# Rotary key by ScalarE, rotary tables by VectorE, first layer's second-attention queries made turned

## The chip, the cores and the metric

The kernel runs on one core of one Trainium2 chip. The metric is the device time of one execution in microseconds (us). Names of engines are those of the profile: PE (TensorE, the matrix engine) with PEld (its weight loads), DVE (VectorE), ACT (ScalarE), POOL (GpSimd), SP (SyncE, which issues the DMAs here). L234 means line 234 of the kernel before; line numbers of the changed kernel differ by up to some 30.

## The reference

A decoder trunk of two layers over one sequence of 256 tokens and 1024 features. Each layer normalises x, projects it once, runs three mixers on parts of the projection (MLA, MoBA and retention), gates and merges them, and adds a squared-ReLU MLP. What matters here:

```
h = rms_norm(x, g)
(cq, ckv, k_rope, mq, mk, mv, ...) = split(h @ w_in)

# first attention, MLA: 8 heads
q = rms_norm(cq) @ w_q_up      -> per head 64 plain + 32 rotary columns
kv = rms_norm(ckv) @ w_kv_up   -> per head 64 plain key + 64 value columns
k = concat(plain key, the one rotary key k_rope, turned by cos/sin, repeated for all heads)
o_mla = softmax(causal(q k^T / sqrt(96))) v

# second attention, MoBA: 8 heads of 64; one block of 256 tokens, so causal attention
q, k = rotary on the first 16 of 64 columns of each head of mq, mk
o_moba = softmax(causal(q k^T / 8)) mv
```

## The kernel before

Data layout. Activations lie "turned" (features on the 128 partitions, 256 tokens along the free dimension) or in "token form" (128 tokens on the partitions). Products are made in fp32r from operands split into a high and a low part: `three` (L234 to L236) issues high x high, high x low, low x high. Every weight block comes by a DMA that SP issues into a buffer `raw` (7 of them), ACT writes its high part `whi` (L213), DVE its low part `wlo` (L215; 6 buffers each). PSUM has eight banks: four for accumulators `acc`, four for all else (`misc`).

Order. The program is a list of units `prog` (one projection block each), and `at(slot, step)` hangs further work behind a unit. `trunk` runs the list, and a scheduler that estimates the time of every instruction then fixes the order on each engine, except where an order is kept by hand (`manual_schedule`, `keep_in_program_order`). The buffers of a pool are given out in rotation, so a change in what is allocated first changes who shares a buffer, or a PSUM bank, with whom.

First layer, start. While x arrives chunk by chunk, `start(k, mq)` (k = 0 to 7) multiplies chunk k by 416 columns for MLA (`b0`: cq, ckv, k_rope) and 512 columns for MoBA's queries (`mq`), in token form: L728, L729 and L731. Ahead of that, WARM = 8 products on constants (L634) run while the first loads come. `moba_done("mq")` scales the two query accumulators by the norm on ACT (L700), and `rope` turns their rotary columns on DVE (L441 to L444, four operations per 128 tokens, with the tables K_COS_MB, K_SIN_MB).

Keys of MoBA, and in the second layer its queries too, are made turned by `project_turned`: per weight block eight products of 512 columns (high weight by both parts of x, L393) and eight of 256 (low weight by the high part, L395); the two halves of the accumulator are added by an ACT copy `second` (L399) and a DVE add into `qkraw` (L400). `rope_turned` (L428 to L430) then multiplies by tables and swaps rows: `swapped` issues four DMAs per pair (L420). For MoBA all three operations run on POOL. `tables` scales the tables by the row of norms, two POOL products of 256 columns (L412), in both layers, and again for retention.

Because the first layer's `mq` are in token form, `moba_turn` (L882, L886) transposes them later, four PE transposes and one ACT copy for each of two groups, ahead of MoBA's scores.

MLA's projections. `c_turn` (L777 to L787) transposes the normalised compressed rows into two PSUM banks `pct`, splits them into `cTh` and `cTl` (L250, L251), and lays the turned rotary key into the key tensor `KK`, one 64-row half at a time: an ACT copy out of PSUM into `krT` (L785), and two DVE copies of it, each repeated for four heads (L786, L787). Then follow the units `qrope` (rotary query columns, copied by ACT as `qr`, L816, swapped by DMA), `qnope` (plain query columns, copied into `Q` by ACT, L801 and L802) and `kvup` (plain keys, copied into `KK` by DVE, L801 and L802 as well, and values `pv`). `qr_rope` (L834 to L838, DVE) turns the rotary query columns and adds them into `Q`. The scores of MLA (L857) need `Q` and `KK`.

## Time and profile before

| | |
|---|---|
| time, median of 3 runs | 835.89 us (835.47 to 836.11) |
| time of the profiled execution | 836.19 us |
| its span, first to last instruction | 834.4 us |
| mean granted TensorE clock | 0.998 |
| PE busy | 827.0 us |
| DVE, ACT, POOL busy | 587.0, 482.3, 93.2 us |
| weights and inputs read | 151.00 MB |

The times come from executions without the profiler, the rows from one execution with it. A row of the timeline has start, duration (us), engine, line, operation, the tile written and the tiles read, shape, and in brackets how long the engine was idle before and what ended that. A row of a group has the number of instructions and their least, median and largest duration in ns. "PE acc L234 <- DVE qkraw L400: 0.4, 1, 0.4" reads: PE at L234 waited for DVE's write of qkraw at L400, 0.4 us in total, once, 0.4 at most. Matmuls are pipelined: their rows overlap, and the distance from start to start is their pace.

### The profile page before, as it was taken

To read this page: it belongs to the slowest core of one execution; us is meant where nothing else is said; L and a number is where in the kernel's file an instruction comes from. 1 tells how busy PE (TensorE), PEld (TensorE's weight loads), DVE (VectorE), ACT (ScalarE), POOL (GpSimd) and SP (SyncE) were. 2 spreads that over 40 slices of the span, in tenths; PEclk is the share of its full clock that TensorE was granted. 3 is DMA by queue.
4 is the path that set the end of the run, shared out by engine and by line. 5 is a ranking of instruction groups with operands and counts; after the bars stand their busy time and mean duration, and the time that the engine had idled before them with its cause. 6 is when DMAs were issued, how large, how long until landed. Compare 5 with 4: busy or idle time off the path is not lost.

```text
span 834.4 us, 12139 instructions
## 1 busy us (share of the span) xinstructions
PE 827.0 (99%) x4366; PEld 701.2 (84%) x4366; DVE 587.0 (70%) x1062; ACT 482.3 (58%) x859; POOL 93.2 (11%) x80
## 2 busy tenths in 40 slices
PE   9999999999999999999999999999999999999997
PEld 7888878888888888888898888888888888888886
DVE  6879667595787666666699876766868775656663
ACT  7766765445556555555685575664545555555552
POOL 0221000040030000000057111002101200000000
PEclk9999999999999999999999999999999999999999
DMA  9956744646467566665565657446565656666611
GB/s 345 361 182 202 242 140 148 192 137 214 145 184 227 184 195 191 189 191 173 172 198 176 211 175 240 155 137 195 156 199 158 219 173 188 200 196 186 197 53 50
DMA packets 45708, 155.98 MB, mean 187 GB/s; under 512 B 5712, under 2 KB 6736, under 8 KB 45392
## 3 DMA queue, kind: packets, MB, share of 16 engines
q1 hardware_dynamic: 45072, 154.54, 58.6%
q8 instruction: 34, 0.56, 0.3%
q10 hardware_dynamic: 576, 0.67, 0.2%
q14 instruction: 26, 0.21, 0.1%
HBM read 151.00 MB, written 1.05 MB: 182 GB/s over the span
## 4 chain that ended last, share of the span: by engine, by line
PE 97%; DMA 1%; DVE 1%; ACT 0%; issue 0%; DVEq 0%
PE acc L234 18%; PE acc L236 18%; PE acc L235 18%; PE pup L1097 14%; PE pup L1099 7%; PE acc L1047 5%; PE acc L393 4%; PE acc L395 2%; PE ps_s L857 1%; PE ps_pt L496 1%; DMA raw<-wts 1%; PE po L523 1%; PE ps_s L462 1%; PE po L525 0%; PE pmt L1013 0%; PE ps_r L462 0%
## 5 line engine op out<-in xcount | busy, mean ns | idle before, releaser
L215 DVE TENSOR_TENSOR wlo<-raw,whi 128x1024 fp32r<-128x1024 f32 (+4 forms) x287 | 347.5, 1219 | 182.4 <-ACT whi L213 126.8
L213 ACT ACTIVATE whi<-raw 128x1024 fp32r<-128x1024 f32 (+4 forms) x287 | 292.4, 1025 | 188.3 <-PE acc L236 104.2
L1097 PE MATMUL pup<-xs,whi 128*128 128x512 f32 x504 | 123.3, 390 | 0.0
L234 PE MATMUL acc<-whi,xs 128*128 128x512 f32 (+1 forms) x304 | 119.6, 395 | 0.0
L236 PE MATMUL acc<-whi,xs 128*128 128x512 f32 (+1 forms) x304 | 119.3, 393 | 0.0
L235 PE MATMUL acc<-wlo,xs 128*128 128x512 f32 (+1 forms) x304 | 118.8, 391 | 0.0
L1097 PEld LDWEIGHTS pup<-xs,whi 128*128 128x128 f32 x504 | 93.4, 188 | 18.6
L234 PE MATMUL acc<-whi,sq 128*128 128x512 f32 x256 | 100.1, 391 | 0.0
L235 PE MATMUL acc<-wlo,sq 128*128 128x512 f32 x256 | 99.9, 390 | 0.0
L236 PE MATMUL acc<-whi,sq 128*128 128x512 f32 x256 | 98.8, 389 | 0.0
L1099 PE MATMUL pup<-xs,wlo 128*128 128x256 f32 x504 | 69.8, 283 | 0.0
L1099 PEld LDWEIGHTS pup<-xs,wlo 128*128 128x128 f32 x504 | 66.7, 191 | 3.1
L234 PEld LDWEIGHTS acc<-whi,xs 128*128 128x128 f32 x304 | 57.1, 188 | 11.9 <-issue 1.3
L236 PEld LDWEIGHTS acc<-whi,xs 128*128 128x128 f32 x304 | 57.1, 188 | 11.5 <-issue 0.3
L235 PEld LDWEIGHTS acc<-wlo,xs 128*128 128x128 f32 x304 | 57.2, 188 | 10.5
L1108 ACT ACTIVATE relu<-relu 128x256 f32<-128x256 f32 x64 | 25.5, 410 | 54.9 <-DVE relu L1107 54.9
L236 PEld LDWEIGHTS acc<-whi,sq 128*128 128x128 f32 x256 | 48.1, 188 | 10.2
L234 PEld LDWEIGHTS acc<-whi,sq 128*128 128x128 f32 x256 | 48.2, 188 | 9.2
L235 PEld LDWEIGHTS acc<-wlo,sq 128*128 128x128 f32 x256 | 48.2, 188 | 8.9
L287 POOL TENSOR_TENSOR sqsum<-sqsum,xsq 128x256 f32<-128x256 f32 x19 | 22.3, 1173 | 290.8 <-issue 170.3
L485 ACT ACTIVATE prob<-prob,smx 128x128 f32<-128x128 f32 x64 | 28.5, 448 | 28.0 <-DVE smx L482 27.9
L393 PE MATMUL acc<-xs,whi 128*128 128x512 f32 x160 | 40.5, 395 | 0.0
(238 smaller groups left out, 1138.1 us busy)
## 6 DMA issues: line engine op xcount, KB each, us to landing
raw<-wts SPq DMA_DIRECT2D x264, 512.0 KB, 4.3
raw<-wts SPq DMA_DIRECT2D x6, 464.0 KB, 8.2
qkoth<-qkraw SPq DMA_DIRECT2D x40, 64.0 KB, 4.4
dec<-consts SPq DMA_DIRECT2D x2, 1024.0 KB, 5.2
raw<-wts SPq DMA_DIRECT2D x4, 416.0 KB, 3.3
xrow<-xtok SPq DMA_DIRECT2D x4, 256.0 KB, 8.0
gn<-gn SPq DMA_DIRECT2D x2, 512.0 KB, 5.8
raw<-wts SPq DMA_DIRECT2D x3, 256.0 KB, 3.9
```

The costliest lines, as they stand in the source:

```text
L213: nc.scalar.activation(hi[:, cs], raw[:, cs], AF.Copy)
L215: nc.vector.tensor_sub(lo[:, cs], raw[:, cs], hi[:, cs].bitcast(F32))
L234: nc.tensor.matmul(o, ah, bh, start=start, stop=False)
L235: nc.tensor.matmul(o, ah, bl, start=False, stop=False)
L236: nc.tensor.matmul(o, al, bh, start=False, stop=stop)
L287: (nc.gpsimd if n < self.on_pool else nc.vector).tensor_add(self.sum, self.sum, sq)
L393: nc.tensor.matmul(acc, wh[:, k, :], xn.both(k), start=k == 0, stop=False)
L485: nc.scalar.activation(p[:, a:b], p[:, a:b], AF.Exp, bias=m[:, 2 + i : 3 + i], scale=scale, accum_out=m[:, 4 + i : 5 + i])
L1047: nc.tensor.matmul(o, a, b, start=half == 0 and i == 0, stop=4 * half + n == KD and i == len(jobs) - 1)
L1097: nc.tensor.matmul(u, w, xm.both(k), start=k == 0, stop=False)
L1099: nc.tensor.matmul(u[:, 0:S], w, xm.k(k)[0], start=False, stop=k == KD - 1)
L1108: nc.scalar.activation(s, s, AF.Square)
```

## The change

It does five things:

- In the first layer, MoBA's queries are made turned, as in the second: `start` accumulates four query blocks in four accumulators (before: two), and the new helper `joins`, taken out of `project_turned`, adds the two halves of each. `moba_turn`, its transposes and the token-form rotary with its tables are gone. The queries are turned by `rope_turned` like the keys, hung behind units 0 and 2 of the second half of MLA's gate projection (`gmla1`).
- In the last step of `start` the first query block is finished ahead of the MLA columns, the others behind them, and the first two loads of key weights are ordered behind the adds.
- The two table products of MoBA become one VectorE operation over both halves (kept in program order); those of retention become one GpSimd operation.
- The rotary key is copied from PSUM into `KK` by two ACT copies; `krT` and the DVE copies are gone.
- WARM is 9 instead of 8.

The constants lose the two tables of the token-form rotary, which moves the offsets of those behind them; that part of the diff is left out.

```diff
--- before.py
+++ after.py
@@ -381,10 +379,27 @@
             xh, xl = xn.k(k)
             three(o, wh[:, k, :], wl[:, k, :], xh, xl, k == 0, k == KD - 1)
 
+    def joins(done):
+
+        pair = []
+
+        def join(n, acc):
+            if n % 2 == 0:
+                pair.append(w2k("qkraw"))
+            second = sb.tile([P, S], F32, name="second", tag="relu", bufs=3)
+            both = nc.scalar.copy(second, acc[:, S : 2 * S]), nc.vector.tensor_add(
+                halves(pair[-1])[:, n % 2, :], acc[:, 0:S], second
+            )
+            if n % 2:
+                done(n // 2, pair[-1])
+            return both
+
+        return join
+
     def project_turned(l, key, xn, done):
 
 
-        pair = []
+        join = joins(done)
 
         def unit(n):
             wh, wl = load_w(l, key, n, 0)
@@ -393,23 +408,17 @@
                 nc.tensor.matmul(acc, wh[:, k, :], xn.both(k), start=k == 0, stop=False)
             for k in range(KD):
                 nc.tensor.matmul(acc[:, 0:S], wl[:, k, :], xn.k(k)[0], start=False, stop=k == KD - 1)
-            if n % 2 == 0:
-                pair.append(w2k("qkraw"))
-            second = sb.tile([P, S], F32, name="second", tag="relu", bufs=3)
-            nc.scalar.copy(second, acc[:, S : 2 * S])
-            nc.vector.tensor_add(halves(pair[-1])[:, n % 2, :], acc[:, 0:S], second)
-            if n % 2:
-                done(n // 2, pair[-1])
+            join(n, acc)
 
         for n in range(4):
             prog.append(((key, n), lambda n=n: unit(n)))
 
-    def tables(xn, tab):
+    def tables(xn, tab, engine):
 
         o = sb.tile([P, 2 * S], F32, name="tab", bufs=1)
-        for i in range(2):
-            cs = slice(S * i, S * i + S)
-            nc.gpsimd.tensor_mul(o[:, cs], tab[:, cs], xn.row)
+        mul = engine.tensor_mul(halves(o), halves(tab), xn.row[:, None, :].to_broadcast([P, 2, S]))
+        if engine is nc.vector:
+            tc.keep_in_program_order(mul)
         return o
 
     def swapped(raw):
@@ -698,9 +707,6 @@
                 dst = mqkv[key] = [w2k(key) for _ in range(NT)]
                 for t in range(NT):
                     nc.scalar.activation(dst[t], accs[t], AF.Copy, scale=xn.col[t])
-                    if key == "mq":
-                        xv = dst[t].rearrange("p (h two r) -> p h two r", h=MB_H, two=2)[:, :, :, 0:8]
-                        rope(xv, K_COS_MB, K_SIN_MB, t, 8, MB_H)
 
             return done
 
@@ -708,29 +714,53 @@
 
             if k == 0:
                 b0.extend(misc_tile("b0") for _ in range(NT))
-                mq.extend(acc_tile() for _ in range(NT))
+                mq.extend(acc_tile() for _ in range(4))
             before(k)
             ah, al = xn.k(k)
             if k == 0:
-
-                blocks = [(mq, slice(0, 256), load_w(l, "mq", 0), 0, True), (mq, slice(256, 512), load_w(l, "mq", 1), 0, False)]
-                blocks.append((b0, slice(0, 416), load_w(l, "b0", 0), 0, True))
+                ws = [load_w(l, "mq", i) for i in range(2)]
+                wq = [[w[:, 0, P * i : P * i + P] for w in two] for two in ws for i in range(2)]
+                wb = [w[:, 0, :] for w in load_w(l, "b0", 0)]
             else:
                 w = load_w(l, "b0mq", k)
-                blocks = [(b0, slice(0, 416), w, 0, False), (mq, slice(0, 512), w, 416, False)]
-
-            for part in ("high", "low"):
-                for accs, cs, w, c, begins in blocks:
-                    ws = slice(c, c + cs.stop - cs.start)
-                    for t in range(NT):
-                        o, sl = accs[t][:, cs], slice(P * t, P * t + P)
-                        if part == "high":
-                            nc.tensor.matmul(o, ah[:, sl], w[0][:, 0, ws], start=begins, stop=False)
-                            nc.tensor.matmul(o, al[:, sl], w[0][:, 0, ws], start=False, stop=False)
-                        else:
-                            nc.tensor.matmul(o, ah[:, sl], w[1][:, 0, ws], start=False, stop=k == KD - 1)
-            if k == KD - 1:
-                moba_done("mq")(mq)
+                wq = [[part[:, 0, 416 + P * n : 416 + P * n + P] for part in w] for n in range(4)]
+                wb = [part[:, 0, 0:416] for part in w]
+
+            def turned_part(part, ns):
+                for n in ns:
+                    if part == 0:
+                        nc.tensor.matmul(mq[n], wq[n][0], xn.both(k), start=k == 0, stop=False)
+                    else:
+                        nc.tensor.matmul(mq[n][:, 0:S], wq[n][1], ah, start=False, stop=k == KD - 1)
+
+            def b0_part(part):
+                for t in range(NT):
+                    o, sl = b0[t][:, :416], slice(P * t, P * t + P)
+                    if part == 0:
+                        nc.tensor.matmul(o, ah[:, sl], wb[0], start=k == 0, stop=False)
+                        nc.tensor.matmul(o, al[:, sl], wb[0], start=False, stop=False)
+                    else:
+                        nc.tensor.matmul(o, ah[:, sl], wb[1], start=False, stop=k == KD - 1)
+
+            if k < KD - 1:
+
+                for part in range(2):
+                    for job in (turned_part, b0_part) if k == 0 else (b0_part, turned_part):
+                        job(part, range(4)) if job is turned_part else job(part)
+            else:
+
+                join = joins(moba_pair("mq"))
+                for part in range(2):
+                    turned_part(part, [0])
+                for part in range(2):
+                    b0_part(part)
+                for n in range(1, 4):
+                    for part in range(2):
+                        turned_part(part, [n])
+
+                have(1)
+                for n in range(4):
+                    behind[l, "mk", 1, 0] = behind[l, "mk", 2, 0] = join(n, mq[n])
 
         qkT = {"mq": {}, "mk": {}}
 
@@ -742,7 +772,7 @@
 
         def moba_rope(key, i):
             if "tab" not in mqkv:
-                mqkv["tab"] = tables(xn, TAB)
+                mqkv["tab"] = tables(xn, TAB, nc.vector)
             qkT[key][i] = rope_turned(mqkv[key, i], mqkv["tab"], nc.gpsimd)
 
         if l:
@@ -781,10 +811,8 @@
             for k in range(3):
                 pt = pts[k // 2][:, (k % 2) * S : (k % 2) * S + S]
                 split(pt, c["h"][:, k, :], c["l"][:, k, :], gain(G_CQ + 3 * l + k))
-            krT = sb.tile([P, S], F32, name="krT", tag="xsq", bufs=2)
-            nc.scalar.activation(krT, pkr, AF.Copy)
-            nc.vector.tensor_copy(KK[0:64, 1::2, :], krT[0:64, None, :].to_broadcast([64, 4, S]))
-            nc.vector.tensor_copy(KK[64:P, 0::2, :], krT[64:P, None, :].to_broadcast([64, 4, S]))
+            nc.scalar.copy(KK[0:64, 1::2, :], pkr[0:64, None, :].to_broadcast([64, 4, S]))
+            nc.scalar.copy(KK[64:P, 0::2, :], pkr[64:P, None, :].to_broadcast([64, 4, S]))
 
         at(slot("mk", 1 if l else 2), c_turn)
 
@@ -847,8 +875,7 @@
         if l == 0:
             at(slot("mv", 3), lambda: tc.keep_in_program_order(nc.sync.dma_start(TAB, consts[:, K_TURNED_MB:])))
         for i in range(2):
-            if l:
-                at(slot("mk", 1 + 2 * i), lambda i=i: moba_rope("mq", i))
+            at(slot("mk", 1 + 2 * i) if l else slot("gmla1", 2 * i), lambda i=i: moba_rope("mq", i))
             at(slot("gmla0", 1 + 2 * i), lambda i=i: moba_rope("mk", i))
         first = slot("mv", 3)
         at(first, lambda: omlaT.extend((t4("omlah"), t4("omlal"))))
@@ -872,19 +899,6 @@
         branch(l, "bmla", omlaT, th_mla, merged)
         first = slot("gmoba1", 1)
         at(first, lambda: omobaT.extend((t4("omobah"), t4("omobal"))))
-
-        def moba_turn(i):
-
-            pt = misc_tile("pq")
-            for a in range(2):
-                for t in range(NT):
-                    k = 2 * i + a
-                    nc.tensor.transpose(
-                        pt[:, (2 * a + t) * P : (2 * a + t + 1) * P], mqkv["mq"][t][:, P * k : P * k + P], ident
-                    )
-            o = sb.tile([P, 2 * S], F32, name="qkT", bufs=4)
-            nc.scalar.copy(o, pt)
-            qkT["mq"][i] = halves(o)
 
         def moba_scores(h0):
             banks = [misc_tile("ps_s") for _ in range(4)][::-1]
@@ -894,9 +908,6 @@
             )
             return banks
 
-        if l == 0:
-            for i in range(2):
-                at(first + 4 * i - 3, lambda i=i: moba_turn(i))
         moba_last = attention(omobaT, None, lambda: mqkv["mv"], MB_D**-0.5, first, moba_scores, mla_last)
 
 
@@ -911,7 +922,7 @@
 
         def ret_pair(i, raw):
             if i == 0:
-                rqkv["tab"] = tables(xn, rqkv["dec"][:, RT_H * 3 * P :])
+                rqkv["tab"] = tables(xn, rqkv["dec"][:, RT_H * 3 * P :], nc.gpsimd)
             rT.append(rope_turned(raw, rqkv["tab"], nc.vector))
 
         rT, or_ps, aT, rg, oret = [], [], {}, {}, []
@@ -1250,7 +1261,7 @@
 
 
 W2K = 17
-WARM = 8
+WARM = 9
 FIRST = 4
 AHEAD = 1
 GAP = 8
```

More of the change, by code (lines that the diff above doesn't have):

```diff
@@ L122 @@
 K_SIN_MLA = K_COS_MLA + NT * 16
-K_COS_MB = K_SIN_MLA + NT * 16
-K_SIN_MB = K_COS_MB + NT * 8
-K_TURNED_MLA = K_SIN_MB + NT * 8
+K_TURNED_MLA = K_SIN_MLA + NT * 16
 K_DEC = K_TURNED_MLA + 2 * S
@@ L1278, in angles @@
         return np.arange(S, dtype=f)[:, None] * inv[None, :].astype(f)
-    for c, s, dim, theta in ((K_COS_MLA, K_SIN_MLA, ROPE, 500000.0), (K_COS_MB, K_SIN_MB, MB_D // 4, 500000.0)):
-        ang = angles(dim, theta)
-        w = dim // 2
-        for t in range(NT):
-            K[:, c + t * w : c + t * w + w] = np.cos(ang[P * t : P * t + P])
-            K[:, s + t * w : s + t * w + w] = np.sin(ang[P * t : P * t + P])
+    ang, w = angles(ROPE, 500000.0), ROPE // 2
+    for t in range(NT):
+        K[:, K_COS_MLA + t * w : K_COS_MLA + t * w + w] = np.cos(ang[P * t : P * t + P])
+        K[:, K_SIN_MLA + t * w : K_SIN_MLA + t * w + w] = np.sin(ang[P * t : P * t + P])
     for c, dim, theta, heads in (
```

## The prediction

> **What bounds the kernel now.** I read the page first: its busy line, the shares of the chain that ended last, and its costliest VectorE group.
>
> ```profile
> PE 827.0 (99%) x4366; PEld 701.2 (84%) x4366; DVE 587.0 (70%) x1062; ACT 482.3 (58%) x859; POOL 93.2 (11%) x80
> ...
> PE 97%; DMA 1%; DVE 1%; ACT 0%; issue 0%; DVEq 0%
> ...
> L215 DVE TENSOR_TENSOR wlo<-raw,whi 128x1024 fp32r<-128x1024 f32 (+4 forms) x287 | 347.5, 1219 | 182.4 <-ACT whi L213 126.8
> ```
>
> TensorE (PE) works for 827.0 us and the chain that ended last is 97% PE. VectorE at 70% and ScalarE at 58% can cost time only through PE, by delivering an operand late or by giving back a PSUM bank late. So each edit is asked two things: does it take work off PE, and does it make or remove a PE wait? The second view is the list of PE's waits (total, times, longest, us).
>
> ```profile
> PE warm L634 <- PEq L1334: 0.8, 1, 0.8
> PE acc L234 <- DVE qkraw L400: 0.4, 1, 0.4
> PE b L728 <- ACT whi L213: 0.2, 1, 0.2
> ```
>
> Three waits, 1.4 us in all, and the first is the start of the program. That nearly caps the gain: whatever moves between ScalarE, VectorE and GpSimd can return only what PE waits for now. The sum is made against the profiled execution, 836.19 us with a span of 834.4; the median of the runs is 835.89, so I take 0.30 off at the end. A measurement of this kernel can tell about 0.2%, 1.67 us, from no change.
>
> **Edit 1: the transposes of the first layer's queries go.** In the chain:
>
> ```profile
> 101.07 0.44 PE pq L882 x4
> 101.51 0.23 PE acc L235
> ```
> ```profile
> 113.36 0.44 PE pq L882 x4
> ```
>
> The two groups of four cost 0.44 us each on PE's own clock, 0.88 together. Queries made turned need none. The products that make them cost PE the same: per 128 rows of x, before, six of 512 columns for two row blocks; after, four of 512 and four of 256, the same count of columns. The new order also splits transposes of the probabilities (L496) into smaller groups, each switch losing about 0.1 of the row above (0.44 for four against 0.35 of pitch); I count 0.16 back. Net on PE's work: -0.72. Two ScalarE copies (L886) go too, off the path.
>
> **Edit 2: one more warm product, and both halves of x for the first product.**
>
> ```profile
> 0.78 3.57 PE L634 MATMUL warm<-const-bfloat16-1.0 128*128 128x512 bf16 x8 [0.78 <-PEq L1334]
> ...
> 9.14 0.62 PE L731 MATMUL acc<-wlo,xs 128*128 128x512 f32 x2
> 9.96 0.46 PE L728 MATMUL b<-whi,xs 128*128 128x416 f32 x1 [0.19 <-ACT whi L213]
> ```
>
> Eight warm products last 3.57 us, so a ninth adds at most 0.45 ahead of the first real product. But PE stands later anyway: the two 512-column products from 9.14 should end their issue at 9.60 (0.23 each, the chain's row) and the next starts at 9.96, held by a weight block. That slack of 0.36 swallows most of it, and the turned products wait for the low half of x as well, which ends about there. Cost 0 to 0.1; 0.45 if the block came earlier.
>
> **Edit 3: the first layer's queries leave ScalarE and VectorE in another shape.**
>
> ```profile
> L700 ACT ACTIVATE mq<-acc,ms x2: 671/674/677, 27.4 to 28.0; 128x512 f32<-128x512 f32 x2
> ...
> L441 DVE TENSOR_TENSOR ropea<-mq,K x2: 284/285/286, 28.8 to 29.8; 128x128 f32<-128x128 f32 x2
> ...
> L399 ACT COPY second<-acc x20: 351/360/389, 32.3 to 553.8; 128x256 f32<-128x256 f32 x20
> ...
> L400 DVE TENSOR_TENSOR qkraw<-acc,second x20: 409/417/425, 34.0 to 557.9; 128x256 f32<-128x256 f32 x20
> ```
>
> Before: two copies of 0.67 on ScalarE and eight rotary operations of up to 0.28 on VectorE. After: four copies of 0.36 and four adds of 0.42. Both engines carry about the same load near 25 to 31 us; the splits of the next weight blocks are queued behind them on both engines and come, by my count of the new order, 1 us or more ahead of PE. The four accumulators that the queries now hold, not two, are free when the adds end, and the first key product follows the first add. Cost 0; with less cover up to 0.4, a copy and a part of an add. The eight swap transfers of the queries go through SP's queue ahead of one weight block that PE uses some 100 us later: nothing.
>
> **Edit 4: tables on VectorE, and six more rotary operations on GpSimd in the first layer.**
>
> ```profile
> L412 POOL TENSOR_TENSOR tab<-TAB,rrow x4: 732/804/897, 36.5 to 438.6; 128x256 f32<-128x256 f32 x4
> ...
> L428 POOL TENSOR_TENSOR qkT<-qkraw,tab x6: 1312/2207/2280, 38.1 to 455.8; 128x512 f32<-128x512 f32 x6
> ```
> ```profile
> 46.00:62.00 16.00, 16.00 (x96) 14.25 (x95) 11.96 (x14) 10.98 (x15) 1.97 (x2) 1.00 0.57 189
> 446.00:460.00 14.00, 13.57 (x83) 11.93 (x82) 12.45 (x11) 9.33 (x14) 11.13 (x6) 1.00 0.63 192
> ```
>
> Two table products of 0.8 on GpSimd become one VectorE operation over 512 columns, some 0.7 by L801 below. GpSimd now also turns the first layer's queries: in the new order it begins four products of 2.2 us in a row when the table is ready, at about 53.4 us, where GpSimd had 1.97 us of work in all from 46 to 62. That matters through the rival below.
>
> **Edit 5: the rotary key goes from PSUM into KK by ScalarE.** In the second layer PE waits behind the old way:
>
> ```profile
> 454.96 0.28 PE L235 MATMUL acc<-cTl,whi 128*128 128x256 f32 x1
> 455.08 0.28 PE L236 MATMUL acc<-cTh,wlo 128*128 128x256 f32 x1
> 455.79 0.39 PE L234 MATMUL acc<-cTh,whi 128*128 128x256 f32 x1 [0.43 <-DVE qkraw L400]
> ```
>
> The pace is 0.12, so the start at 455.79 is 0.59 late. VectorE shows why:
>
> ```profile
> 447.74 2.00 DVE L215 TENSOR_TENSOR wlo<-raw,whi 128x1024 fp32r<-128x1024 f32 x1 [0.46 <-ACT whi L213]
> 449.67 1.78 DVE L786 COPY KK<-krT 64x1024 f32<-64x1024 f32 x1
> 451.46 1.70 DVE L787 COPY KK<-krT 64x1024 f32<-64x1024 f32 x1
> ...
> 455.32 0.41 DVE L400 TENSOR_TENSOR qkraw<-acc,second 128x256 f32<-128x256 f32 x1
> ```
>
> Two copies of krT, 3.5 us, stand ahead of the adds that PE waits for; GpSimd is busy for 11.13 of these 14 us, and operations with SBUF operands are stretched (wlo 2.00 against its mean of 1.22). Without the copies the adds come 3 us earlier: the 0.59 goes. What is late next there is the copy of Q's first half, with slack. Gain 0.59.
>
> In the first layer the same edit puts two 64x1024 copies on ScalarE.
>
> ```profile
> L786 DVE COPY KK<-krT x2: 678/1228/1778, 46.7 to 449.7; 64x1024 f32<-64x1024 f32 x2
> ...
> L785 ACT ACTIVATE krT<-pct x2: 372/374/375, 45.5 to 447.6; 128x256 f32<-128x256 f32 x2
> ...
> L801 ACT COPY Q<-acc x4: 580/581/582, 49.9 to 458.5; 64x512 f32<-64x512 f32 x4
> ...
> L801 DVE COPY KK<-acc x4: 675/680/683, 57.0 to 469.0; 64x512 f32<-64x512 f32 x4
> ...
> L802 DVE COPY KK<-acc x4: 694/695/696, 57.6 to 469.7; 64x512 f32<-64x512 f32 x4
> ```
>
> No row shows a 64x1024 copy from PSUM by ScalarE. Two 64x512 ones (0.58) would be 1.16; the same copy took VectorE 0.68 with a free port and 1.78 without. Bounds 0.6 and 1.8; I take 1.05, near the double of the nearest row. krT's 0.37 goes. So ScalarE gets 1.7 us more just ahead of Q's copies:
>
> ```profile
> 44.15 0.48 ACT L250 ACTIVATE cTh<-pct,GX 128x256 fp32r<-128x256 f32 x1 [1.57 <-DVE cTl L251]
> 44.52 1.05 ACT L213 ACTIVATE whi<-raw 128x1024 fp32r<-128x1024 f32 x1
> ...
> 49.39 0.56 ACT L816 COPY qr<-pqr 128x512 f32<-128x512 f32 x1
> ```
>
> Counting the products of the new order at the rows' pace, the transposes into pct end at about 47.0, not 42. ScalarE then runs three cTh (0.4 each, the third waits for VectorE), from 48.2 two copies to 50.3, two weight splits to 52.4, qr to 53.0 and Q's first two copies to 54.2.
>
> ```profile
> 54.17 0.28 PE L234 MATMUL acc<-cTh,whi 128*128 128x256 f32 x1
> ...
> 54.88 0.28 PE L234 MATMUL acc<-cTh,whi 128*128 128x256 f32 x1
> ...
> 55.60 0.40 PE L234 MATMUL acc<-whi,xs 128*128 128x512 f32 x1
> ```
>
> The two halves of the key up-projection (six products each) start at 54.17 and 54.88 and follow without a gap. In the new order they begin at about 54.15, so Q's copies, whose bank the first half takes, cost 0.0 to 0.2. But the second half now takes the bank of the first, with nothing between them on PE: it waits until VectorE has made both copies of the first half. From the issue of the first half's last product: its own 0.28, then 0.68 and 0.69, 0.1 for two signals (the add that ends at 455.73 lets PE go on at 455.79), less the pace of 0.12: 1.63. Ahead of the copies on VectorE stand the table and one wlo, which ends between 54.7 (1.22) and 55.7 (stretched), against products that end at 55.2: 0 to 0.4 more. I take 1.8 for the whole, bounds 1.3 and 2.4.
>
> **Sum.** -0.72 + 0.05 - 0.59 + 1.8 = +0.54: 836.73 for such an execution, 836.4 beside the median. Forecast: no change that can be told.
>
> **The rivals.** (a) *The new wait does not show*: something stands between the halves, or the bank is free in time. Then -1.3: 834.6, still within 0.2%. To be faster by more than that, 1.67 would have to come back; 0.88 of transposes and 0.59 of wait, 1.47, is all I find, and the rest would have to come from weight blocks split earlier, of which PE's waits show no need.
>
> (b) *GpSimd's four products hold VectorE*, and it comes out slower. The stretched rows (+0.8 on a wlo, +1.1 on a copy from SBUF) happen where GpSimd works without pause. In the first layer that will be 53.4 to 62, and on VectorE there stand wlo, two copies, wlo, qr's two products, two copies, the additions into Q, and then the first scores on PE. Q's products also wait for a transfer:
>
> ```profile
> 49.98 2.48 SPq L420 DMA_DIRECT2D qkoth<-qr  x4
> ```
> ```profile
> 55.75 0.69 DVE L834 TENSOR_TENSOR qr<-qr,K 128x512 f32<-128x512 f32 x1 [2.37 <-DMA qkoth<-qr]
> ```
>
> From the issue at 49.98 to its use at 55.75 pass 5.8 us; with qr ready at 53.0 that is 58.8. Two products of 1.7, two copies of 0.7 and an addition then end at 64.3, and PE wants the scores at about 65.1 with the stall counted. If the swap lands 0.8 later, or one more operation is stretched, PE waits again. Four operations stretched by 1.0 more, less the slack of 0.8, and the 0.4 at the halves: 836.4 + 0.4 + 1.4 = 838.2. For it: the sizes of the stretched rows. Against: the copies that free the bank read PSUM, and those rows stay at 0.68 throughout. It decides from about 59.6 for the landing.
>
> The Trainium skill, page "SBUF — State Buffer", section "SBUF: two separate sides", says that VectorE and GpSimd hold a shared pair of ports exclusively for a whole instruction, if VectorE's operation reads two operands from SBUF or runs in a two-port mode, and that ScalarE has ports of its own. By that rule the new table product and the wlo behind it could be shut out for up to a whole 2.2 us product, which speaks against the move to VectorE and for (b), with the same 838.2; the stretched wlo, and PSUM copies that are not, agree with it so far.
>
> (c) *ScalarE's 64x1024 copies are dear.* Each 0.1 us above 1.05 puts Q's copies, and so the first half, 0.2 later. At 1.75 apiece: +1.4, 837.8; it is slower by 0.2% from about 1.65 each. The double of 0.58 speaks against.
>
> **Chances and range.** Forecast 0.52, (a) 0.14, (b) 0.19, (c) 0.07, and 0.08 for more than I can find in gains. Faster by over 0.2%: 0.10, the 0.08 and a little of (a). Slower: 0.27, (b), (c) and the forecast's own upper tail. The same: 0.63. The forecast by itself spans 835.7 to 837.3. The range reaches down past (a), to 834.5, and up to (b), 838.3.
>
> **What would show it.** Right: no L882 rows; PE's waits list one on KK's copy (L829 or L830 in the new numbering) of 1.3 to 2 us near 55 us, and none on qkraw near 455; KK from pct on ScalarE at 1.0 to 1.2; KK from acc at 0.68. Wrong: a second PE wait at the first scores near 65 (b), KK copies from pct above 1.6 (c), no wait between the halves (a), or a change at places that the edits do not touch.

## The result and the profile after

The changed kernel takes 837.49 us (median of 21 runs, 837.12 to 838.71) against 835.94 us (21 runs, 834.86 to 836.92): a ratio of 1.0020, 95% interval 1.0014 to 1.0026. It is slower by 1.55 us, and 1 lies outside the interval; the forecast was 836.4 within 834.5 to 838.3, no change that can be told. Its profiled execution took 837.12 us with a span of 835.3; beside the 836.19 and 834.4 of before that is 0.93 more in time, where the sum said 0.54.

The busy line and the chain's shares on the page of the profile after:

```profile
span 835.3 us, 12153 instructions
...
PE 826.2 (99%) x4369; PEld 701.0 (84%) x4369; DVE 586.5 (70%) x1056; ACT 484.7 (58%) x861; POOL 98.7 (12%) x80
...
PE 98%; ACT 1%; DVE 0%; DMA 0%; issue 0%; ACTq 0%; DVEq 0%
```

PE does 0.8 us less than before (827.0): the transposes of L882 are gone from the trace. Yet the span is longer, so PE waits more. The list of PE's waits (total, times, longest, us):

```profile
PE acc L232 <- DVE KK L830: 1.6, 1, 1.6
PE warm L643 <- PEq L1343: 0.8, 1, 0.8
PE ps_pt L505 <- ACT probT L507: 0.4, 1, 0.4
PE acc L732 <- DVE xs L276: 0.2, 1, 0.2
```

The wait for qkraw in the second layer is gone, as forecast. A wait of 1.6 us for KK's copy (L830, the one of 64 upper rows) is new, as forecast. A third, 0.4 us for the transposes of the probabilities, was not forecast. The new wait in the timelines of PE, of VectorE and of ScalarE:

```profile
53.70 0.39 PE L234 MATMUL pv<-whi,cTl 128*128 128x512 f32 x1
54.19 0.39 PE L232 MATMUL acc<-cTh,whi 128*128 128x256 f32 x1
...
54.89 0.28 PE L234 MATMUL acc<-cTh,wlo 128*128 128x256 f32 x1
56.74 0.35 PE L232 MATMUL acc<-cTh,whi 128*128 128x256 f32 x1 [1.58 <-DVE KK L830]
```

```profile
55.21 0.68 DVE L829 COPY KK<-acc 64x512 f32<-64x512 f32 x1 [1.18 <-PE acc L234]
55.91 0.69 DVE L830 COPY KK<-acc 64x512 f32<-64x512 f32 x1
```

```profile
47.92 1.01 ACT L814 COPY KK<-pct 64x1024 f32<-64x1024 f32 x1
48.94 1.01 ACT L815 COPY KK<-pct 64x1024 f32<-64x1024 f32 x1
...
53.55 0.58 ACT L830 COPY Q<-acc 64x512 f32<-64x512 f32 x1
...
56.18 0.58 ACT L830 COPY Q<-acc 64x512 f32<-64x512 f32 x1
```

The first half of the key up-projection begins at 54.19, the second at 56.74 instead of 0.12 after 54.89: 1.73 late. VectorE idles until the first half is done (1.18 us), makes the two copies of 0.68 and 0.69, and PE goes on when the second ends. That is the step that was worked out as 1.63, 0.1 longer. ScalarE's two 64x1024 copies from PSUM took 1.01 each (1.05 was taken), and Q's first copies end at 54.13 (54.2 was worked out). Note the last row of ScalarE: Q's second copies end at 56.76, just when PE goes on.

The unforecast place, timelines of PE, VectorE, ScalarE and GpSimd:

```profile
84.95 0.61 PE L505 MATMUL ps_pt<-K,prob 128*128 128x128 f32 x3 [0.44 <-ACT probT L507]
```
```profile
81.25 2.32 DVE L213 TENSOR_TENSOR wlo<-raw,whi 128x1024 fp32r<-128x1024 f32 x1
...
83.68 1.39 DVE L499 TENSOR_SCALAR prob<-prob,smx 128x128 f32<-128x128 f32 x2
```
```profile
83.50 1.05 ACT L211 ACTIVATE whi<-raw 128x1024 fp32r<-128x1024 f32 x1
84.45 0.48 ACT L507 ACTIVATE probT<-ps_pt 128x384 f32<-128x384 f32 x1
```
```profile
81.06 1.43 POOL L439 TENSOR_TENSOR qkT<-qkT,qkoth 128x512 f32<-128x512 f32 x1
82.45 2.27 POOL L438 TENSOR_TENSOR qkoth<-qkoth,tab 128x512 f32<-128x512 f32 x1
```

PE starts the probability transposes 0.61 over its pace. Two things come late. What ended last is ScalarE's copy probT of the transposes before, done at 84.93, which stands behind a weight split in ScalarE's own queue. Nearly as late are the probabilities to be transposed: VectorE brings them in two operations (83.68), the second done at 85.07, after a wlo of 2.32, stretched from its mean of 1.22. The two operations take 1.39 together, where the same two take 0.55 in a_norope (81.35), a kernel below in which GpSimd is idle at that time. In after GpSimd works from 77.07 to 86.20 almost without a pause: first two operations on keys, as in before, then four of the six that edit 4 adds for the first layer's queries.

To see where each kernel gains and loses, the trace is cut where MoBA's last score in the first layer begins (133.61 us before, 135.27 after). All kernels have the same products still to come there, and have done the same ones but for the form of the start and the transposes of the queries.

| profile | up to the first layer's last score | from there to the last product | up to the last product | ratio of medians, 95% |
|---|---|---|---|---|
| after | +1.66 | -0.79 | +0.87 | 1.0020 (1.0014 to 1.0026) |
| a_half | +2.87 | -0.82 | +2.05 | 1.0023 (1.0014 to 1.0032) |
| a_norope | +3.45* | -0.83 | +2.62 | 1.0016 (1.0008 to 1.0025) |
| a_spread | +3.46* | -0.80 | +2.66 | 1.0014 (1.0005 to 1.0023) |
| a_cfirst | +2.98 | -0.81 | +2.17 | 1.0032 (1.0020 to 1.0045) |
| c_norope | +0.55 | -0.83 | -0.28 | 0.9997 (0.9988 to 1.0006) |
| c_spread | +0.25 | -0.97 | -0.72 | 0.9994 (0.9985 to 1.0003) |
| a_ropev | +4.40* | -0.96 | +3.44 | 1.0051 (1.0039 to 1.0064) |
| a_turn | +3.57 | +0.11 | +3.68 | 1.0047 (1.0035 to 1.0060) |
| a_krt | +0.87 | +2.93* | +3.80 | 1.0038 (1.0025 to 1.0052) |
| b_kk | -0.21 | -1.25 | -1.46 | 0.9989 (0.9980 to 0.9998) |
| b_tab | +0.11 | +0.98 | +1.09 | 1.0034 (1.0021 to 1.0048) |
| b_kktab | -0.50 | -1.01 | -1.51 | 0.9989 (0.9980 to 0.9998) |

Differences are to before, in us, of one profiled execution each; the ratios are of the runs. The start, up to the first product behind the keys, ends between 0.5 earlier and 0.7 later than in before, so a single entry of the first column is not better than that. An entry with * holds some 1.7 us of halved clock behind a PE wait, told below, which not every run has.

### The profile page after: what moved, and what is told of

The parts are those of the page before. It is cut to its first block, busy times and chain, and to the rows that moved or that the text cites. A ratio compares the mean times of both kernels' runs of the same rounds, so it can differ in the third digit from the quotient of the medians.

```text
span 835.3 us, 12153 instructions
## 1 busy us (share of the span) xinstructions
PE 826.2 (99%) x4369; PEld 701.0 (84%) x4369; DVE 586.5 (70%) x1056; ACT 484.7 (58%) x861; POOL 98.7 (12%) x80
## 3 DMA queue, kind: packets, MB, share of 16 engines
HBM read 150.98 MB, written 1.05 MB: 182 GB/s over the span
## 4 chain that ended last, share of the span: by engine, by line
PE 98%; ACT 1%; DVE 0%; DMA 0%; issue 0%; ACTq 0%; DVEq 0%
PE acc L232 18%; PE acc L234 18%; PE acc L233 18%; PE pup L1108 14%; PE pup L1110 7%; PE acc L1058 5%; PE acc L408 4%; PE acc L410 2%; PE ps_pt L505 1%; PE ps_s L884 1%; PE po L532 1%; PE acc L732 1%; PE ps_s L471 1%; PE acc L734 0%; PE pmt L1024 0%; PE po L534 0%
```

## The experiments

### Take the wait away: a_half

The second half of the keys gets a bank of the other four, so that it need not wait for the copies of the first. (In the trace this half then also comes first, at 48.95.)

```diff
-                acc = acc_tile()
+                acc = misc_tile("kacc") if l == 0 and len(ks) == 1 and b else acc_tile()
```

> The changed kernel, with one edit: the second half of the first layer's key up-projection accumulates in a bank of the other PSUM group, so that the halves no longer share one. Theory (the shared bank): the wait of 1.6 us on KK near 55 us goes, and with it about that much of the time: ratio to before 1.000 (0.999 to 1.0005), some 1.6 us under the changed kernel. Rival (GpSimd's longer work holds VectorE, and the bank only shows it): the time lost moves to the first scores or to the transposes of probabilities near 84 us, ratio stays at 1.0015 or above.

Measured: 838.17 us, ratio 1.0023, not faster than the change itself. The list of PE's waits:

```profile
PE ps_pt L505 <- DVE prob L499: 1.0, 2, 0.7
PE acc L232 <- ACT Q L830: 1.0, 1, 1.0
...
PE ps_pt L505 <- ACT th L570: 0.7, 1, 0.7
```

The wait for KK is gone and 1.0 us for Q's second copies stands next to its place: the product behind the halves (acc<-whi,xs at 56.87) needs them done. They end where the wait on the bank had ended, as the ScalarE rows of after show. So in this order the bank by itself is worth some 1.73 - 1.0 = 0.7. Moreover the probability transposes now wait 1.0 and 0.7 instead of 0.4. The theory that this bank holds the loss, at its whole price, falls.

### Take GpSimd's extra work away: a_norope and a_spread

a_norope leaves the rotation of the first layer's queries out; a_spread keeps it and hangs it behind a later unit. Its six operations then run at 80.03 and from 92.36 to 99.8, still beside the first attention's softmax, but beside other rows of it.

```diff
# a_norope
-            qkT[key][i] = rope_turned(mqkv[key, i], mqkv["tab"], nc.gpsimd)
+            if l == 0 and key == "mq":
+                qkT[key][i] = halves(mqkv[key, i])
+            else:
+                qkT[key][i] = rope_turned(mqkv[key, i], mqkv["tab"], nc.gpsimd)
# a_spread
-            at(slot("mk", 1 + 2 * i) if l else slot("gmla1", 2 * i), lambda i=i: moba_rope("mq", i))
+            if l:
+                at(slot("mk", 1 + 2 * i), lambda i=i: moba_rope("mq", i))
...
+        if l == 0:
+            for i in range(2):
+                at(slot("gmoba0", 2 * i), lambda i=i: moba_rope("mq", i))
...
-        engine.tensor_mul(halves(o), halves(raw), cos)
+        mul = engine.tensor_mul(halves(o), halves(raw), cos)
+        if late:
+            tc.keep_in_program_order(mul)
```

> The changed kernel without the rotary turn of the first layer's queries (left out: GpSimd's six operations and eight swap transfers; the queries go unturned into the scores). Everything else stays, the shared bank too. Theory B (GpSimd holds VectorE): the wait of 0.6 us on the transposes of probabilities near 84 us goes; the bank's wait of 1.6 to 1.7 us near 55 us stays, since it consists of copies out of PSUM: ratio 1.0005 to 1.0015. Rival (VectorE is short of time by itself): both waits stay, ratio 1.002.

> The changed kernel, all of its work kept, with GpSimd's operations on the first layer's queries put behind those on the keys, at a later unit, so that two products and not four run in a row from about 53 us. Theory B: VectorE is stretched less from 57 to 62 us, where it does not bound anything; the bank's wait stays, the later operations meet the softmax: ratio 1.001 to 1.0025.

Measured: 836.61 and 836.67 us, ratios 1.0016 and 1.0014. In both traces the wait near 84 us is gone and the 1.6 us near 55 is as it was. So the 84 us wait comes from those GpSimd operations at that place, and the one near 55 does not. (The order on ScalarE and PE changes there too, so these runs do not part the late probT from the late probabilities.) By their ratios the two lie 0.3 to 0.5 us under the change (intervals overlap), and both are still slower than before.

Their profiled executions took 838.85 and 838.91, though, as did one more run of each; the other nine lie at 836.1 to 837.0. PE's wait, and PE's stretches around it (from:to, length, PE busy, granted clock, DMA share, GB/s), in a_norope:

```profile
PE acc L232 <- DVE KK L833: 1.6, 1, 1.6
```
```profile
56.50:57.60 1.10, 0.00 (x0) 1.00 0.56 142
...
58.00:61.30 3.30, 3.30 (x12) 0.50 0.50 122
61.30:64.00 2.70, 2.70 (x13) 0.98 0.80 317
```

Right after the wait of 1.6 us the granted clock is 0.50 for these 3.3 us and 0.98 over the next 2.7, so some 3.4 us ran at half. Half of that is lost, 1.7 us, the larger part of the 2.2 by which these runs stand above the median. The profile of a_spread shows the same. The second long run of each has no profile; its mean clock of 0.997, where the other nine have 0.998 to 1.000, speaks for the same cause. In the profiled execution of after the same wait was not followed by that:

```profile
56.80:60.20 3.40, 3.40 (x18) 1.00 0.53 124
```

The Trainium skill, page "TensorE: Matmul & The Clock Gate", section "Part 1: The HAM clock gate", says that the clock is halved after an idle window of about 3.4 us and is full again after about 3.4 us of work. The some 3.4 us at 0.50 agree with the second; a gap of 1.6 us that was enough in the two profiled executions is less than the first.

### Bring the late chain forward: a_cfirst, c_norope, c_spread

Why do the two halves meet without work between them? The transposes into pct come at 44.6 to 45.6 in after, at 38.7 and 41.2 to 42.0 in before. ScalarE in after:

```profile
27.49 3.49 ACT L211 ACTIVATE whi<-raw 128x1024 fp32r<-128x1024 f32 x4
30.86 0.43 ACT L680 ACTIVATE junk<-c 128x256 f32<-128x256 f32 x1
...
32.21 0.42 ACT L680 ACTIVATE junk<-c 128x256 f32<-128x256 f32 x1
...
35.33 0.32 ACT L680 ACTIVATE junk<-c 128x128 f32<-128x128 f32 x1
```

Four splits of weight blocks stand ahead of the first square (L680) and one ahead of each later one; the last square is at 35.33, before it was at 32.90. The norms and the transposes follow from these squares. a_cfirst orders five of the blocks behind them.

```diff
-                    nc.scalar.activation(junk[:, :n], ct[:, cs], AF.Square, scale=n**-0.5, accum_out=m[:, i : i + 1])
+                    square = nc.scalar.activation(junk[:, :n], ct[:, cs], AF.Square, scale=n**-0.5, accum_out=m[:, i : i + 1])
+            if l == 0:
+                for key in ((l, "mk", 2, 0), (l, "mk", 3, 0), (l, "qrope", 0), (l, "mv", 0), (l, "qnope", 0)):
+                    behind[key] = (*behind.get(key, ()), square)
```

> The changed kernel with one thing put first: in the first layer the four squares of the compressed columns (L680) are issued by ScalarE ahead of the splits of the key and query weights, not among them. Theory A (late chain: turned queries push those squares behind four weight splits, so the transposes into pct come 3.4 to 6 us later than before, and everything between pct and the key up-projection has no slack): pct starts at 38 to 40 us, no wait near 55, ratio to before 0.9980 to 0.9990, some 2.5 to 3 us under the changed kernel. Theory B (GpSimd's six more operations hold VectorE): pct is early, but waits of 1 us or more stay between 50 and 90 us, ratio at or above 1.000.

Measured: 838.58 us, ratio 1.0032. The transposes into pct now begin at 32.7, 5.9 us earlier than even in before, and the wait near 55 is gone. PE's waits:

```profile
PE ps_s L887 <- DVE KK L832: 2.1, 1, 2.1
...
PE ps_pt L505 <- DVE prob L499: 0.8, 1, 0.8
```

The wait moved to the first scores, near 63 us. VectorE and GpSimd there:

```profile
60.97 1.69 DVE L869 TENSOR_TENSOR Q<-qr,qkoth 64x512 f32<-64x512 f32 x1
62.67 1.70 DVE L868 TENSOR_TENSOR Q<-qr,qkoth 64x512 f32<-64x512 f32 x1
64.38 0.69 DVE L869 TENSOR_TENSOR Q<-qr,qkoth 64x512 f32<-64x512 f32 x1
64.99 0.68 DVE L832 COPY KK<-acc 64x512 f32<-64x512 f32 x1
```
```profile
53.46 6.95 POOL L437 TENSOR_TENSOR qkT<-qkraw,tab 128x512 f32<-128x512 f32 x4 [22.76 <-DVE tab L419]
...
62.19 1.62 POOL L439 TENSOR_TENSOR qkT<-qkT,qkoth 128x512 f32<-128x512 f32 x1
```

Q's additions, two operands from SBUF, take 1.69 and 1.70 while GpSimd works, and 0.69 right after it stops at 63.8; then comes the copy of KK (from PSUM, 0.68) for which PE waits. This is rival (b), its mechanism and its place, in a kernel where the halves' wait is not. The expectation that went with the late chain as the cause falls.

If that is so, the early chain must pay once GpSimd's work is away from there. c_norope is a_cfirst with the edit of a_norope (it leaves the same rotation out), c_spread is a_cfirst with the edit of a_spread (it keeps all of the work).

> The changed kernel with the squares of the compressed columns first, and without the rotary turn of the first layer's queries (left out as in the kernel before this one). Here the halves have banks of their own and the transposes into pct are early. Theory B: the waits at the first scores (2.2 us) and near 87 us (0.9 us), which stood behind stretched operations of VectorE, go, and the 0.9 us of transposes shows at last: ratio 0.9970 to 0.9990. Rival (VectorE's own order or load is late): a wait of over 1 us stays between 50 and 90 us, ratio above 1.000.

> As the kernel before this one, with the squares of the compressed columns first (halves in banks of their own, transposes into pct early). Theory B: with two products of GpSimd in a row and not four, VectorE's products and additions for Q are stretched by 3 to 4 us less, the wait of 2.2 us at the first scores goes or falls under 0.7; later waits up to 1 us where the other operations meet the softmax: ratio 0.9980 to 1.0005. Rival (VectorE's own order): the wait at the first scores stays above 1.5 us, ratio above 1.002.

Measured: 835.44 and 835.52 us, ratios 0.9997 (0.9988 to 1.0006) and 0.9994 (0.9985 to 1.0003). Neither can be told from before, and c_norope missed the gain that was expected of it. GpSimd's timeline in c_spread:

```profile
53.73 3.56 POOL L437 TENSOR_TENSOR qkT<-qkraw,tab 128x512 f32<-128x512 f32 x2 [22.76 <-DVE tab L419]
58.94 1.31 POOL L440 TENSOR_TENSOR qkoth<-qkoth,tab 128x512 f32<-128x512 f32 x1 [1.65 <-DMA qkoth<-qkraw]
```

It has 3.56 us of products there instead of 6.95, is free from 57.3 to 58.9, and no PE wait but that of the program's start is left. So the two causes together, the late chain with its bank and GpSimd's products, account for the loss, and removing either alone leaves most of it or moves it. The time is still not under that of before by what the 0.88 of transposes promise. In c_spread the 36 transposes of the probabilities up to the last score cost 3.92 us, from start to start, where they cost 3.41 before. Most of that, 0.42, stands at two groups (73.57 and 76.75): their first two transposes take 0.26 and 0.17 instead of 0.11, and each begins some 0.05 behind the end of VectorE's operation on its probabilities. GpSimd is idle then, so it is not the cause. These are waits too short for the list. The rest, about 0.6 of the first column, is no more than starts differ by and stays open.

### Put the query rotation on VectorE: a_ropev

```diff
-            qkT[key][i] = rope_turned(mqkv[key, i], mqkv["tab"], nc.gpsimd)
+            qkT[key][i] = rope_turned(mqkv[key, i], mqkv["tab"], nc.vector if l == 0 and key == "mq" else nc.gpsimd)
```

> The changed kernel with two of the three rotary operations of the first layer's queries on VectorE instead of GpSimd; the late transposes into pct are left as they are. Theory A: Q's copies are still late on ScalarE, a wait of 0.7 to 1.7 us near 55 us stays, ratio 1.001 to 1.003. Theory B: GpSimd has two products instead of four in a row, VectorE's operations near 55 to 62 and 80 to 86 us are not stretched, ratio 0.9990 to 1.000.

Measured: 840.12 us, ratio 1.0051, the slowest. PE's waits, and a row of VectorE:

```profile
PE acc L232 <- ACT Q L830: 1.6, 1, 1.6
PE acc L232 <- DVE KK L830: 1.1, 1, 1.1
```
```profile
54.27 3.44 DVE L437 TENSOR_TENSOR qkT<-qkraw,tab 128x512 f32<-128x512 f32 x2
```

That is 2.7 us of waits instead of 1.6 and 0.4. The two moved products stand on VectorE ahead of KK's copies, which begin at 57.63: the 1.1 us is the price of the move. The 1.6 us is for Q's second copies on ScalarE, the same that a_half met, and they are late with or without the move. The granted clock is 0.50 from 60 to 62 us behind these waits.

### The edits one at a time: a_turn, a_krt, b_kk, b_tab, b_kktab

Three of them start from the kernel before: b_kk has the rotary key copied by ScalarE alone, b_tab the tables on VectorE (and those of retention as one GpSimd operation) alone, b_kktab both. Two start from the change: a_krt takes the ScalarE copies back, a_turn keeps the turned queries alone.

```diff
# b_kk (in a_krt and a_turn the other way)
-            krT = sb.tile([P, S], F32, name="krT", tag="xsq", bufs=2)
-            nc.scalar.activation(krT, pkr, AF.Copy)
-            nc.vector.tensor_copy(KK[0:64, 1::2, :], krT[0:64, None, :].to_broadcast([64, 4, S]))
-            nc.vector.tensor_copy(KK[64:P, 0::2, :], krT[64:P, None, :].to_broadcast([64, 4, S]))
+            nc.scalar.copy(KK[0:64, 1::2, :], pkr[0:64, None, :].to_broadcast([64, 4, S]))
+            nc.scalar.copy(KK[64:P, 0::2, :], pkr[64:P, None, :].to_broadcast([64, 4, S]))
# b_tab (in a_turn the other way, and there WARM = 8)
-        for i in range(2):
-            cs = slice(S * i, S * i + S)
-            nc.gpsimd.tensor_mul(o[:, cs], tab[:, cs], xn.row)
+        mul = engine.tensor_mul(halves(o), halves(tab), xn.row[:, None, :].to_broadcast([P, 2, S]))
+        if engine is nc.vector:
+            tc.keep_in_program_order(mul)
```

> The kernel before with one part of the change: the rotary key goes from PSUM into KK by two ScalarE copies. The halves of the key up-projection lie in two banks here. Theory (shared bank): ScalarE's copies cost PE nothing, the second layer's wait on qkraw goes: -0.6 us, ratio 0.9993 (0.9985 to 1.000). Rival (ScalarE's queue made late): a PE wait on Q or KK near 50 to 55 us and a ratio above 1.0005.

Measured: 835.09 us, ratio 0.9989. No PE wait is left but that of the program's start. ScalarE's copies alone are a gain: 1.25 us from the last score of the first layer on, where 0.59 was forecast for the change. Of it 0.73 comes at the place of the wait on qkraw, and 0.48 at the second layer's first scores. In before these begin at 468.27, right behind KK's first copy on VectorE (467.54, 0.68 long), a wait too short for the list that the forecast did not see.

> The kernel before with only the tables of the second attention moved to VectorE, in both layers. Theory A: the two norms of the compressed columns on GpSimd do not stand behind table products in either order here, so the first layer does not change; in the second layer VectorE has one operation more ahead of the copies of krT, and the wait on qkraw or at the first scores grows by 0.7 to 2.5 us: ratio 1.001 to 1.003. Rival: GpSimd is free earlier, VectorE is stretched less, ratio 0.999 to 1.000.

Measured: 838.97 us, ratio 1.0034 (runs of 837.30, 837.55, 838.97, 839.16 and 839.40). Its trace has one new wait, in the second layer, at 467 us:

```profile
PE ps_s L857 <- DVE KK L801: 1.7, 1, 1.7
```

VectorE's and GpSimd's rows ahead of it:

```profile
460.57 1.67 DVE L837 TENSOR_TENSOR Q<-qr,qkoth 64x512 f32<-64x512 f32 x1
```
```profile
461.65 3.45 POOL L430 TENSOR_TENSOR qkT<-qkT,qkoth 128x512 f32<-128x512 f32 x2
```

The place is the one that was expected, the way there another. The table is made on VectorE at 449.51, behind krT's two copies; on GpSimd, in before, it was ready at 439.29. So GpSimd's rotation begins at 450.28 and runs to 465.10, and beside it three of Q's four additions, ahead of KK's copies, take 1.67 to 1.70. In before GpSimd is done at 460.27 and they take 0.69 at most. krT's copies and the table do not push KK's copies themselves, since VectorE is idle for 0.92 us behind them, before 458.05.

> The kernel before with both moves, the rotary key by ScalarE and the tables by VectorE, and the first layer's queries left in token form. Theory A: the cost of the change lies in the turned queries alone, so this is at or under the key alone: ratio 0.9985 to 0.9995. Rival (the moves disturb one another): ratio at or above 1.000, with a wait near 455 to 470 us.

Measured: 834.87 us, ratio 0.9989. The first of Q's additions here:

```profile
461.88 0.69 DVE L835 TENSOR_TENSOR Q<-qr,qkoth 64x512 f32<-64x512 f32 x1
```

With krT gone from VectorE the table is made at 444.93, GpSimd is done at 460.17, before Q's additions begin, and the table costs nothing that the medians show. b_kk and b_kktab are the versions that beat both kernels, and cannot be told from each other.

> The changed kernel with the rotary key back on the way of before (krT by ScalarE, two copies by VectorE); the buffers then come out so that the two halves lie in two banks. Theory (shared bank): no KK wait near 55 us (-1.6), but the second layer's wait on qkraw near 455 us is back (+0.6): ratio to before 1.0005 to 1.001. Rival (ScalarE's copies themselves delay Q and so PE): the time also falls, but no wait on qkraw is needed for it, and a kernel with ScalarE's copies alone would be slower than before.

Measured: 839.15 us, ratio 1.0038. No wait for KK is left near 55 us, as expected, and the first layer has lost only 0.9, two waits of 0.7 on ScalarE's copies included. The second has lost 2.9, not at the wait on qkraw that was expected but at the same place as b_tab:

```profile
PE ps_s L886 <- DVE KK L831: 2.0, 1, 2.0
```

Behind that wait of 2.0 us the granted clock in this profile is 0.87 from 470.5 to 472, 0.50 to 474 and 0.74 to 476: 0.2, 1.0 and 0.5 us, 1.7 in all. Without it the second layer has lost 1.2, much as in b_tab.

> Only the first layer's queries made turned; rotary key and tables as before, eight warm products. The halves lie in two banks here. Theory: eight transposes less, -0.7 us, the wait on qkraw near 455 us stays: ratio 0.9992 (0.9985 to 1.000). Rival (GpSimd's six more rotary operations hold VectorE): waits of 0.4 us or more on the softmax between 69 and 90 us or at the first scores, ratio 1.000 to 1.001.

Measured: 839.93 us, ratio 1.0047, worse than the theory and its rival had it. The longest PE wait (from 47.0 to 48.7 us; the next are 0.7, 0.7 and 0.4), and the timelines of GpSimd and VectorE ahead of it:

```profile
PE acc L233 <- DVE wlo L213: 1.7, 1, 1.7
```
```profile
39.08 2.07 POOL L421 TENSOR_TENSOR tab<-TAB,rrow 128x256 f32<-128x256 f32 x2 [18.07 <-DMA TAB<-consts]
41.11 0.70 POOL L690 TENSOR_TENSOR ssc<-ssc,neghalf 128x2 f32<-128x2 f32 x1
...
43.04 0.75 POOL L690 TENSOR_TENSOR ssc<-ssc,neghalf 128x2 f32<-128x2 f32 x1
```
```profile
41.85 1.64 DVE L699 TENSOR_SCALAR c<-c,ssc,ms 128x256 f32<-128x256 f32 x2 [1.66 <-POOL ssc L690]
...
46.36 2.30 DVE L213 TENSOR_TENSOR wlo<-raw,whi 128x1024 fp32r<-128x1024 f32 x1
```

With the tables on GpSimd its queue stands still until their load has come, and then holds two table products (2.07) and a product of 1.3 ahead of the small powers of the norms (L690). These begin at 41.11 and 43.04; in after, with nothing ahead of them, the first begins at 36.56. VectorE idles 1.66 us for the norms, and the wlo for which PE waits stands behind them. So the move of the tables, which alone is a loss, is what keeps the turned queries from losing 3.6 us in the first layer: with it (a_krt) they lose 0.9.

## Why the prediction was right, and where it was not

Right, with what was measured:

- The transposes are gone (0.88 off PE), and the wait for qkraw: from the last score on, after gains 0.8 where 0.59 was forecast.
- The wait between the halves: 1.73, and the first half 0.26 late, 1.99 for the 1.8 taken. Its chain, two copies of 0.68 and 0.69 behind the first half's end, is the one worked out from rows of before. b_kk confirms the second layer's step on its own, and shows a second gain there that the sum did not have.
- Rival (c) did not happen: ScalarE's 64x1024 copies cost 1.01 each.
- Edits 2 and 3 show no cost in this pair: the first product behind the keys begins at 36.38, in before at 36.60. But over the profiles with the same products ahead of it, it begins between 36.38 and 37.32 with the new start and between 36.10 and 36.72 with the old. So the 0 to 0.1 stays open, some tenths are possible, and that after gains 0.22 here is luck.

Wrong or missed:

- The point: +0.5 was forecast and +1.55 measured, a change that 21 runs can tell from none. The forecast by itself spanned 835.7 to 837.3, and 837.49 lies above that; it is in the range only because the range reaches up to (b).
- The step "six more rotary operations on GpSimd" named the right mechanism, stretched VectorE operations, and priced it at one place only, the first scores. There it just missed: Q's first two additions end at 64.87 and the scores begin at 65.26. The four products took 6.91 there, not 8.8, so GpSimd was done at 63.29, before the additions. It cost 0.61 at the softmax near 84 us, which no term held: the row of operations was not followed to its end. a_norope and a_spread show whose it is, a_cfirst shows the mechanism at the place that was named.
- The price of rival (b) does not come out of its own words: four operations stretched by 1.0, less a slack of 0.8, are 3.2, not the 1.4 that was added. With 3.2 it would be 840.0, outside the range.
- Rival (a) took the halves' wait as one that can simply be absent, for -1.3. a_half shows that behind it stood 1.0 for Q's copies. What a removed wait is worth was taken as its length.
- The sum closes when the terms are put at their measured sizes: -0.88 for the transposes, -0.22 at the start, +1.99 and +0.61 make +1.50, and 0.16 is left to the +1.66 up to the last score; -0.8 behind it makes +0.9. The sum had 0.16 for smaller groups of transposes, but the probabilities' transposes cost 3.44 from start to start where they cost 3.41 before, so that the two 0.16 agree is luck. The missed 0.61 is partly hidden by 0.27 at the start and 0.2 behind the last score that came out better than summed.
- The median moved by 1.55, the profiled execution by 0.93. 0.25 is before's profiled execution standing above its median, and 0.37 after's being the fastest of its 21. Seven of the 21 lie at 837.88 to 838.71. Three of these have the mean clock of 0.997 of a_norope's long runs, so a clock halved after the 1.6 us wait would fit them; three others have 0.999, as the short runs do. No profile of this kernel caught such an execution, so it stays open.

The Trainium skill, page "SBUF — State Buffer", section "SBUF: two separate sides", with its exclusive hold for a whole GpSimd instruction, agrees with the rows of a_cfirst and after. Additions of 0.69 took 1.69, which is 1.0 more and less than the 1.74 of GpSimd's product beside them. KK's copies from PSUM stayed at 0.68 and 0.69 in after (55.21 and 55.91), beside GpSimd's four products (52.98 to 59.89).

## What to carry to other kernels

Price a wait by what stands behind it: look up when the next operand or bank that the same consumer needs is ready before a removed wait is counted as gain. A move between engines has one price per place: ScalarE's key copies gained 1.25 us, the VectorE tables alone lost 1.0 in the second layer, and the two together lost nothing, since the table then stood earlier in VectorE's queue and GpSimd was done earlier. So try the parts alone and together before the whole is kept or dropped. When an engine that shares a path with another gets more work, follow that work to its last instruction, and read every operation of the other engine beside it, not only those at the place one is watching.

## What was not expected of the hardware

A PE gap of 1.6 us was enough in 2 of 11 executions of a_norope, and in 2 of 11 of a_spread, to add 2.2 us; in the profiled one of each the granted clock was 0.50 for some 3.4 us right behind it. The profiles of a_krt and a_ropev show 0.50 behind waits of 2.0 and of 1.6 with 1.1, those of after (1.6), a_turn (1.7), b_tab (1.7), a_cfirst (2.1) and a_half (1.0) none. b_tab has three of its five runs 1.4 to 2.1 us above the other two, at a mean clock of 0.997 against 0.999. So a wait of that length costs its own time and, in some executions, about as much again.
